# Decoder layer on one core: the last six attention pieces' places, the stores at the second set's end, and the time of the embedding's inputs

## The chip, the core and the metric

The kernel runs on one core of a Trainium2 chip. The core has five engines that each work through their own instructions in order: PE (TensorE, matrix products; PEld is its loading of weights), DVE (VectorE), ACT (ScalarE), POOL (GpSimd) and SP (SyncE, which here only issues DMAs; in the profile SPq). DMAs are issued by SP and by POOL. The metric is the device time of one execution in microseconds, lower is better.

## What is computed

One layer of a decoder on 1024 tokens of 2048 channels. Cut to what matters:

```python
h = x @ w_in + b_in                                # 2048 -> q, k, v, g_attn, u_pool, g_pool
q, k, v, g_attn, u_pool, g_pool = split(h)
a = banded_sink_attention(q, k, v, sinks, bias, valid) * silu(g_attn)
b = multiscale_pool(u_pool, w_pool, pool_scale) * silu(g_pool)
mix = concat([a, b]) @ w_out
ple = sigmoid(x @ w_gate_ple) * (p @ w_ple)        # p: 1024 x 256, the layer's embedding
out = layer_norm(ALPHA * x + mix + ple, ln_gain, ln_bias)
```

The attention looks back over 128 tokens, in blocks of 128 queries against 256 keys, with 16 heads of 64 channels; `ple` is the part for which the embedding's inputs `p` are needed. All inputs and outputs are float32.

## The kernel before

**Products.** All large matrix products are made by a scheme of seven products instead of eight for a 2 x 2 split of the blocks (`ALONE`, `BESIDE` give the order, p1 to p7). Each of the seven is one call of `product` (L464): four blocks of three matmuls (`mm3`, L180 to L186: high weights by high inputs, high by low, low by high), since float32 is split into a high and a low part. The product's weights are split by ACT (`wh`, the cast of L824) and by DVE (`wl`, the subtraction of L126), four products ahead (`take`, `units_to`), from a ring of five `raw` buffers that SP fills. For p5 and p6 DVE first makes sums and differences of the raw blocks (`three_sums`, `make_unit`). PE writes to the banks `qa` and `qb`, two of each; ACT copies a first result to a `part` tile (L424), DVE adds later ones to it (L126).

**The clock.** `run_group` counts a tick after each product. `after(n, fn)` puts `fn` into the program n products later, `later(n, fn)` does so behind the work that was marked last. So the order on each engine is fixed when the program is written, by these numbers; an engine that has to wait holds up all that stands behind it in its row.

**The sets.** The input projection is made in sets of groups for half of the input channels each: the first half's results go to DRAM as `h` (`keep`, store by SP through `load`, L139), and are added to the second half's by a DMA that POOL issues (`finished`, L432). Set 2 ends at about 675 us of the profiled execution; its last groups store `h_110` to `h_115`. Set 3 follows and takes the gate of the embedding in (`w_gate_ple`) too.

**Attention.** `heads` (L579) makes one of 16 pieces: two blocks (n = 0, 1) of two pairs of heads, spread over the products of set 2. Per block `score` (L620, eight matmuls `sc`), `softmax` (L639) and `share` (L649) on ACT, `trans` (L656, four transposes `tr`), a masked copy by POOL (L663), and `value` (L672, four matmuls `pv`, or two for a sequence's first block), whose two halves DVE adds. The pieces start nine products apart, the last six eight apart. With nine, one piece's `score` falls into the same place between two products as the `trans` and `value` of another; with eight they fall into four or five.

**Centred weights.** `centre_weights` (L947) reads the output weights as 32 cells of 256 KB (`cw`), subtracts a mean on DVE and stores them as `wc`, by SP; a later `cw` load waits for the store that frees its buffer.

**The embedding's inputs.** `embed_in` (L889) asks for four blocks of `p` at 1, 3, 5 and 7 products behind its start (DMA by SP, 256 KB, tile `s`, in_p), and nine behind it splits all four: a cast by ACT (L901) and a subtraction by DVE (L126, `self.lo`) each. The parts are used by `embed` (L913) about four products behind that. It is started in set 3 by

```python
            if self.groups[g + i + 1][0][0].b[0] == 4 and i < n3 - 2:
                self.after(5, self.embed_in)
```

Of the kernel before, what the change touches and what calls it, by code (L numbers as in the profile page):

```python
# [33 lines left out]
H = 4 * P  # L34
# [31 lines left out]
class Layer:  # L66
# [203 lines left out]
    def two(self):  # L270
        return self.tile(self.twos, [P, 2, self.F], "two")
# [304 lines left out]
        self.ident_act(c, c, self.b8[:, j : j + 1], 0.125)  # L576
        self.load(self.qd[j], c.rearrange("p h t -> p (h t)"))

    def heads(self, h, j, half):  # L579

        nc, g = self.nc, j // 4
        st = self.tile(self.sm, [P, 64], "st")
# [44 lines left out]
        def shift(n):  # L627
            f = slice(4 * n, 4 * n + 4)
            sink = self.c(C_SINK + 8 * j, 16).rearrange("p (i b e) -> p i b e", i=2, b=4)[:, :, block(n)]
            nc.vector.tensor_scalar(out=neg[:, f], in0=mx[:, f], scalar1=-1.0, scalar2=None, op0=ALU.mult)  # L630
            self.tt(sk[:, f].rearrange("p (i e) -> p i e", i=2), sink, neg[:, f].rearrange("p (i e) -> p i e", i=2), ALU.add)
            nc.scalar.activation(sk[:, f], sk[:, f], AF.Exp)
# [18 lines left out]
        def trans(n):  # L651
            ps = self.bank("tr", 1)
            for i in range(2):
                for e in range(2):
                    o = (2 * i + e) * P
                    nc.tensor.transpose(ps[:, o : o + P], sc[n, i][:, e, P:], self.ident)  # L656
            hi, lo = pt[n] = [self.slot(F32R)[:, :T] for _ in range(2)]
            nc.scalar.copy(out=hi, in_=ps)
            self.lo(lo, ps, hi)
            if not none(n):  # L660
                old[n] = [self.slot(F32R)[:, :T] for _ in range(2)]
                for a, t in zip(old[n], pt[n]):
                    nc.gpsimd.affine_select(out=a.rearrange("p (c q) -> p c q", c=4), in_=t.rearrange("p (c q) -> p c q", c=4).bitcast(F32), pattern=[[0, 4], [-1, P]],  # L663
                                            compare_op=ALU.is_ge, fill=0.0, base=-1, channel_multiplier=1)

        def value(n):
            ps = self.bank("pv", 1)
            ms = [(self.vv[h][:, block(n)], t) for t in pt[n]]
            if not none(n):
                ms += [(self.vd[h][:, block(n) - 1 + h], t) for t in old[n]]  # L670
            for i, (w, t) in enumerate(ms):
                nc.tensor.matmul(ps, w, t, start=i == 0, stop=i == len(ms) - 1)  # L672
            if not pre:
                pre.append(two(self.slot()[:, :T]))
            low = self.slot()[0:64, :T]
            nc.scalar.copy(out=low, in_=ps[64:128])
            hi, low = (t.rearrange("p (i e q) -> p i e q", i=2, e=2) for t in (ps[0:64], low))
            for e in range(2):
                self.tt(pre[0][64 * e : 64 * e + 64, :, n * P : n * P + P], hi[:, :, e], low[:, :, e], ALU.add)
            if n:  # L680
                f = slice(h * T + 256 * half, h * T + 256 * half + 256)
                for i in range(2):
                    (self.aside if last else self.load)(self.pre[j + i][:, f], pre[0][:, i])
# [4 lines left out]
        for n in range(2):  # L688
            for i in range(2):
                self.after(6 + 4 * n, lambda n=n, i=i: score(n, i))  # L690
            self.after(9 + 4 * n, lambda n=n: shift(n))
            self.after(15 + 4 * n, lambda n=n: trans(n))
            for i in range(2):
                self.after(10 + 4 * n, lambda n=n, i=i: softmax(n, i))
                self.later(12 + 4 * n, lambda n=n, i=i: share(n, i))
            self.after(19 + 5 * n, lambda n=n: value(n))


    def gate_ahead(self, j):
# [247 lines left out]
    def centre_weights(self, at, by):  # L947

        nc = self.nc
        cells = [(b, h) for b in range(NB) for h in range(2)]  # L950
        sums = self.fix.tile([P, 8, NB], F32, name="wsum")
        mean = self.fix.tile([P, 8], F32, name="wmean")
        now, cws = [], [self.cw, self.cw2]

        def fetch(b, h):
            cws.append(cws.pop(0))
            now.insert(0, self.load(self.tile(cws[0], [P, H], "cw"), self.wout[b, 0][:, h * H : h * H + H]))

        def add_up(b, h):
            k = now.pop().rearrange("p (k m) -> p k m", k=4)  # L960
            nc.vector.reduce_sum(sums[:, 4 * h : 4 * h + 4, b : b + 1], k, axis=mybir.AxisListType.X)

        def take_mean():
            nc.vector.reduce_sum(mean.rearrange("p (k b) -> p k b", b=1), sums, axis=mybir.AxisListType.X)
            nc.vector.tensor_scalar(out=mean, in0=mean, scalar1=1.0 / D, scalar2=None, op0=ALU.mult)

        def centre(b, h):
            w = now.pop()
            k = w.rearrange("p (k m) -> p k m", k=4)
            m = mean[:, 4 * h : 4 * h + 4].rearrange("p (k m) -> p k m", m=1).broadcast_to([P, 4, P])  # L970
            self.tt(k, k, m, ALU.subtract)
            self.load(self.wc[b, 0][:, h * H : h * H + H], w)

        for step in (add_up, centre):
            for c in cells:
                self.after(at, lambda c=c: fetch(*c))
                self.later(at + 3, lambda c=c, step=step: step(*c))
                at += by if step is centre and c[0] % 3 else 2
            if step is add_up:
                self.later(at + 2, take_mean)  # L980
                at += 2
# [114 lines left out]
    def run(self):  # L1096
# [29 lines left out]
        flat = lambda c: c.rearrange("p h t -> p (h t)")  # L1126
        halves = lambda t: t.rearrange("p (h t) -> p h t", h=2)
        store = lambda w: hid if w is win else gat
# [4 lines left out]
        def keep(where):  # L1133
            return lambda b, c: self.load(where[b], flat(c))

        def kept_part(where):
            return lambda b: halves(where[b])
# [19 lines left out]
        def jobs(todo, half, first, done, tokens=2 * T, ahead=None):  # L1157
            return [Job(w, b0, b1, half, first(w), done(w), tokens, ahead=ahead) for w, b0, b1 in todo]

        s1 = jobs(qkv, 0, lambda w: None, lambda w: keep(hid))  # L1160
        s2 = jobs(qkv, 1, lambda w: kept_part(hid), lambda w: finish)
        s2 += jobs(rest, 1, lambda w: None, lambda w: keep(store(w)))
        s3 = jobs(rest, 0, lambda w: kept_part(store(w)), consume)
        for j in s3:
            j.wait = 8 if j is s3[-1] else 7 if j is s3[-2] else 5 if j in s3[-4:] else 4
# [144 lines left out]
        t = 9  # L1310
        self.after(5, lambda: build_kv(KB, self.k_build, 0))
        self.after(6, lambda: build_kv(VB, self.v_build, 0))
        for i in range(16):
            self.after(t - 2 + 9 * i - max(0, i - 10), lambda i=i: self.heads(i // 2 % 2, i // 4 * 2, i % 2))
        for h, n in enumerate((65, 77)):
            self.after(t + n, lambda h=h: build_kv(KB, self.k_build, 1, (h,)))
        for h in range(2):
# [11 lines left out]
        for i in range(n3):  # L1329
            if i == 1:  # L1330
                over.close()
                work.close()
                work, over = ExitStack(), ExitStack()
                self.slot_n = T + 16
                self.slots = self.work_pool("slots", 16, work)
                self.extras = self.work_pool("e2", 6, over)
            if self.groups[g + i + 1][0][0].b[0] == 4 and i < n3 - 2:
                self.after(5, self.embed_in)
                self.after(7, lambda: self.embed_w(2))
            if i == n3 - 2:  # L1340

                over.close()
                work.close()
                work = ExitStack()
                self.slot_n = T
                six[:] = 5 * [pp] + 3 * [self.work_pool("p8", 3, work)]
                self.slots = self.work_pool("slots1", 8, work)
                self.twos = self.work_pool("twos1", 4, work)
                self.new_part = part_of_six
                for n, b in enumerate(s3[-4].b + s3[-3].b):  # L1350
                    self.after((1, 1, 5, 6)[n], lambda b=b: self.gate_ahead(b - GA0))
                pooled()
                for n, step in enumerate(make_pooled):
                    (self.later if n > 4 else self.after)((10, 13, 16, 19, 22, 27, 30)[n], step)
                for n, b in enumerate(b for j in s3[-2:] for b in j.b):
                    self.after(16 + 2 * n, lambda b=b: self.gate_ahead(b - GA0))
            first = self.groups[g + i][0][0]
            if first.w is wgate and first.b[0] in (4, 6, 8, 10):
                self.pool_sums(*divmod(first.b[0] // 2 - 2, 2), kept_pool)
            self.run_group(g + i, () if i else steps)  # L1360
# [3 lines left out]
        half = F1 // 2  # L1364
# [181 lines left out]
```

## Time and profile before

| | us |
|---|---|
| median of 3 runs | 1440.29 |
| lowest, highest | 1440.24, 1440.69 |
| profiled execution, its own time | 1439.74 |
| span of its profile | 1438.0 |
| PE busy | 1425.3 |
| DVE busy | 1114.3 |
| ACT busy | 791.4 |
| POOL busy | 234.5 |
| mean granted clock of PE | 0.996 |

The span goes from the first to the last instruction, all times below are counted from its start. A row of the timeline has start, duration, engine, line, operation, output<-input and count, and in brackets the idle time ahead of it with what ended it. The rows of issues have, per kind of DMA, the count, the size and the median time from issue to landing.

### The profile page before, as it was taken

Reading aid. Unit: us, or ns where it says so; the run is one execution under the profiler, and the core shown is the slowest. Engines: PE = TensorE matmul, PEld = TensorE weight load, DVE = VectorE, ACT = ScalarE, POOL = GpSimd, SP = SyncE. Lnnn points to the kernel's source line nnn. Section 1 sums busy time; section 2 is a strip of 40 time slices with the busy share of each in tenths; the row PEclk is TensorE's granted clock in tenths of the full one; section 3 lists DMA queues with packets and bytes.
Section 4 is the critical chain, followed back from the end, with each engine's and each line's share of the span. In section 5 each row is a group of like instructions: output and inputs, shape, how many; then the busy total and the mean of one; then the engine's idle time right before and its main releaser. Section 6 shows DMA issues by size and latency. Waiting matters only on the chain.

```text
span 1438.0 us, 20364 instructions
## 1 busy us (share of the span) xinstructions
PE 1425.3 (99%) x6824; PEld 1207.9 (84%) x6824; DVE 1114.3 (77%) x2044; ACT 791.4 (55%) x1564; POOL 234.5 (16%) x342
## 2 busy tenths in 40 slices
PE   9999999999999999999999999999999999999996
PEld 7888888888888888888888888888888888899996
DVE  7859578878888887887778876957677666987787
ACT  6546377565766666666565444443455533655476
POOL 0000202211221221221011211211000211111223
PEclk9999999999999999999999999999999999999998
DMA  9463886555556555548787869998799677494476
GB/s 360 186 239 117 235 227 212 168 182 170 173 187 205 192 182 190 193 149 282 207 248 216 222 205 292 341 279 255 201 300 314 193 204 230 134 280 117 117 238 232
DMA packets 119034, 311.86 MB, mean 217 GB/s; under 512 B 13585, under 2 KB 27025, under 8 KB 118929
## 3 DMA queue, kind: packets, MB, share of 16 engines
q1 hardware_dynamic: 94192, 229.82, 46.7%
q0 software_dynamic: 21408, 73.41, 21.6%
q10 hardware_dynamic: 3328, 7.34, 1.5%
q8 instruction: 53, 0.87, 0.3%
q14 instruction: 53, 0.43, 0.1%
HBM read 211.95 MB, written 98.57 MB: 216 GB/s over the span
## 4 chain that ended last, share of the span: by engine, by line
PE 98%; POOL 0%; ACT 0%; issue 0%; DMA 0%; DVE 0%; POOLq 0%; SPq 0%; DVEq 0%; ACTq 0%
PE qa L183 17%; PE qa L185 16%; PE qa L184 16%; PE qb L183 12%; PE qb L185 12%; PE qb L184 12%; PE sc L620 2%; PE pv L672 2%; PE sc L185 1%; PE sc L183 1%; PE sc L184 1%; PE tr L656 1%; PE tr L877 1%; PE pv L877 1%; DMA two<-in_p 0%
## 5 line engine op out<-in xcount | busy, mean ns | idle before, releaser
L824 ACT CAST wh<-raw 128x512 fp32r<-128x512 f32 x428 | 264.7, 620 | 412.3 <-PE qa L184 147.2
L126 DVE TENSOR_TENSOR wl<-raw,wh 128x512 fp32r<-128x512 f32 x428 | 295.9, 695 | 109.1 <-ACT wh L824 104.0
L424 ACT COPY part<-qa 128x512 f32<-128x512 f32 (+1 forms) x180 | 103.7, 576 | 82.4 <-PE qa L185 81.1
L126 DVE TENSOR_TENSOR part<-part,qb 128x512 f32<-128x512 f32 (+1 forms) x120 | 81.1, 676 | 48.6 <-PE qb L185 43.1
L183 PE MATMUL qa<-b11h,wh 128*128 128x512 f32 (+2 forms) x292 | 109.0, 373 | 0.0
L183 PE MATMUL qb<-b21h,wh 128*128 128x512 f32 (+2 forms) x292 | 108.9, 373 | 0.0
L185 PE MATMUL qa<-b11h,wl 128*128 128x512 f32 (+2 forms) x292 | 108.7, 372 | 0.0
L184 PE MATMUL qa<-b11l,wh 128*128 128x512 f32 (+2 forms) x292 | 108.5, 372 | 0.0
L185 PE MATMUL qb<-b21h,wl 128*128 128x512 f32 (+2 forms) x292 | 108.5, 372 | 0.0
L184 PE MATMUL qb<-b21l,wh 128*128 128x512 f32 (+2 forms) x292 | 108.4, 371 | 0.0
L183 PE MATMUL qb<-t1h,wh 128*128 128x512 f32 (+1 forms) x260 | 100.3, 386 | 0.0
L183 PE MATMUL qa<-t2h,wh 128*128 128x512 f32 (+1 forms) x260 | 100.0, 385 | 0.0
L183 PE MATMUL qa<-t3h,wh 128*128 128x512 f32 (+1 forms) x260 | 100.0, 385 | 0.0
L183 PE MATMUL qa<-t4h,wh 128*128 128x512 f32 (+1 forms) x260 | 99.8, 384 | 0.0
L185 PE MATMUL qb<-t1h,wl 128*128 128x512 f32 (+1 forms) x260 | 99.7, 384 | 0.0
L183 PE MATMUL qb<-b22h,wh 128*128 128x512 f32 (+1 forms) x260 | 99.7, 384 | 0.0
L185 PE MATMUL qa<-t2h,wl 128*128 128x512 f32 (+1 forms) x260 | 99.7, 383 | 0.0
L185 PE MATMUL qa<-t3h,wl 128*128 128x512 f32 (+1 forms) x260 | 99.7, 383 | 0.0
L185 PE MATMUL qb<-b22h,wl 128*128 128x512 f32 (+1 forms) x260 | 99.7, 383 | 0.0
L185 PE MATMUL qa<-t4h,wl 128*128 128x512 f32 (+1 forms) x260 | 99.6, 383 | 0.0
L184 PE MATMUL qb<-t1l,wh 128*128 128x512 f32 (+1 forms) x260 | 99.5, 383 | 0.0
L184 PE MATMUL qb<-b22l,wh 128*128 128x512 f32 (+1 forms) x260 | 99.5, 383 | 0.0
(336 smaller groups left out, 3488.8 us busy)
## 6 DMA issues: line engine op xcount, KB each, us to landing
raw<-in_win SPq DMA_DIRECT2D x65, 512.0 KB, 4.3
h<-part SPq DMA_DIRECT2D x34, 512.0 KB, 3.5
part<-h POOLq DMA_DIRECT2D x34, 512.0 KB, 7.0
cw<-in_wout SPq DMA_DIRECT2D x64, 256.0 KB, 3.3
raw<-in_wgate SPq DMA_DIRECT2D x32, 512.0 KB, 5.0
raw<-wc SPq DMA_DIRECT2D x32, 512.0 KB, 4.4
s<-in_x SPq DMA_DIRECT2D x44, 256.0 KB, 6.0
s<-in_rel SPq DMA_DIRECT2D x32, 256.0 KB, 3.8
```

Of the source, the lines that this page charges most:

```text
L126: return (eng or self.nc.vector).tensor_tensor(out=out, in0=a, in1=b, op=op)
L183: mm(ps, wh, xh, start=start, stop=False, skip_group_check=True)
L184: mm(ps, wh, xl, start=False, stop=False, skip_group_check=True)
L185: return mm(ps, wl, xh, start=False, stop=stop, skip_group_check=True)
L424: self.mark("ACT", self.nc.scalar.copy(out=dst, in_=ps))
L620: nc.tensor.matmul(ps[:, e, z:], q, kk[:, keys], start=k == 0, stop=k == 1)
L656: nc.tensor.transpose(ps[:, o : o + P], sc[n, i][:, e, P:], self.ident)
L672: nc.tensor.matmul(ps, w, t, start=i == 0, stop=i == len(ms) - 1)
L824: ins = self.nc.scalar.copy(out=out, in_=a)
L877: mm = self.nc.tensor.matmul(ps[b], w[u][:, b, k], self.ple_p[v][:, 2 * h + k], start=k + u + v == 0, stop=k + v == 2, skip_group_check=True)
```

## The change

Three edits. `heads` gets a fourth argument `by`, the distance to the next piece: nine for pieces 0 to 9, where nothing changes (15 and 19 products, 19 and 24 come out as before), eight for the last six: `trans` at 14 and 18 products instead of 15 and 19, `value` at 18 and 22 instead of 19 and 24. The stores of the last three groups of set 2 (`h_110` to `h_115`, 512 KB each) and of the last four cells of `wc` (256 KB each) are issued by POOL (`aside`) instead of SP (`load`). And `embed_in` starts three products ahead in place of five, so that its loads and its splits come two products sooner.

```diff
-    def heads(self, h, j, half):
+    def heads(self, h, j, half, by):
...
-            self.after(15 + 4 * n, lambda n=n: trans(n))
+            self.after(by + 6 + 4 * n, lambda n=n: trans(n))
...
-            self.after(19 + 5 * n, lambda n=n: value(n))
+            self.after(by + 10 + (by - 4) * n, lambda n=n: value(n))
...
-            self.load(self.wc[b, 0][:, h * H : h * H + H], w)
+            (self.aside if (b, h) in cells[28:] else self.load)(self.wc[b, 0][:, h * H : h * H + H], w)
...
         s2 += jobs(rest, 1, lambda w: None, lambda w: keep(store(w)))
+        for j in s2[-3:]:
+            j.done = lambda b, c, where=store(j.w): self.aside(where[b], flat(c))
...
-            self.after(t - 2 + 9 * i - max(0, i - 10), lambda i=i: self.heads(i // 2 % 2, i // 4 * 2, i % 2))
+            self.after(t - 2 + 9 * i - max(0, i - 10), lambda i=i: self.heads(i // 2 % 2, i // 4 * 2, i % 2, 9 - (i > 9)))
...
-                self.after(5, self.embed_in)
+                self.after(3, self.embed_in)
```

The changed file has two lines more behind L1162, so the lines that the rows name stay as they are.

On PE, at the first of the last six pieces, between two products of set 2 (`qa`, `qb`; the numbers are those of the tiles), in the program before:

```order
L185 MATMUL qa_5159<-t4h_1519,wl_5279 128x512
L672 MATMUL pv_5395<-s_5213,v_986_4708 128x512
L672 MATMUL pv_5395<-s_5214,v_986_4708 128x512
L672 MATMUL pv_5395<-s_5217,d_987_4709 128x512
L672 MATMUL pv_5395<-s_5218,d_987_4709 128x512
L656 MATMUL tr_5406<-ident,s_5088 128x128 x2
L656 MATMUL tr_5406<-ident,s_5096 128x128 x2
```

and in the changed one, one product sooner:

```order
L185 MATMUL qb_5282<-b22h_1475,wl_5252 128x512
L656 MATMUL tr_5345<-ident,s_5088 128x128 x2
L656 MATMUL tr_5345<-ident,s_5096 128x128 x2
L620 MATMUL sc_5369<-kh_1771,s_5272 128x256
L620 MATMUL sc_5369<-kl_1772,s_5272 128x256
```

The four transposes (two rows of two) of the shares `s_5088` and `s_5096` have moved from behind the value product to the place ahead of it, where another piece's scores stand.

On POOL, at the end of set 2, in the program before (the masked copies, the last attention results `pre`, and set 3's first instruction):

```order
L663 AFFINE_SELECT s_6836<-s_6832 128x512
L663 AFFINE_SELECT s_6958<-s_6954 128x512
L663 AFFINE_SELECT s_6959<-s_6955 128x512
L145 DMA pre_162<-s_6944 128x256
L145 DMA pre_163<-s_6944 128x256
L724 MEMSET s_7536 128x16
```

and in the changed one, from the second of the four `wc` stores on:

```order
L145 DMA wc_244<-cw_6796 128x512
L663 AFFINE_SELECT s_6939<-s_6935 128x512
L663 AFFINE_SELECT s_6940<-s_6936 128x512
L145 DMA wc_245<-cw_6899 128x512
L145 DMA h_112<-part_6697 128x1024
L145 DMA h_114<-part_6699 128x1024
L145 DMA wc_245<-cw_6960 128x512
L145 DMA pre_162<-s_6925 128x256
L145 DMA pre_163<-s_6925 128x256
L145 DMA h_113<-part_6698 128x1024
L145 DMA h_115<-part_6700 128x1024
L724 MEMSET s_7536 128x16
```

The stores of `wc` and `h` have come into POOL's row between its last masked copies and the results `pre`; on SP they are gone.

On ACT, in set 3, where the embedding's inputs are split (e and s from L901 are their high parts, the tiles right of the arrow the inputs; `wh` are weights, `part` copies of PE's results), in the program before:

```order
L154 CAST s_9137<-s_9041 128x512
L824 CAST wh_9165<-raw_8741 128x512
L424 COPY part_9047<-qa_9052 128x512
L901 CAST e_9216<-s_8999 128x512
L824 CAST wh_9189<-raw_8741 128x512
L824 CAST wh_9241<-s_1880_9184 128x512
L901 CAST e_9220<-s_9066 128x512
L424 COPY part_9239<-qa_9245 128x512
L901 CAST s_9228<-s_9160 128x512
L901 CAST e_9224<-s_9113 128x512
```

and in the changed one:

```order
L154 CAST s_9139<-s_9043 128x512
L901 CAST e_9162<-s_8960 128x512
L824 CAST wh_9181<-raw_8741 128x512
L901 CAST e_9166<-s_9001 128x512
L901 CAST s_9174<-s_9115 128x512
L901 CAST e_9170<-s_9068 128x512
L424 COPY part_9049<-qa_9054 128x512
L424 COPY part_9239<-qa_9245 128x512
L824 CAST wh_9205<-raw_8741 128x512
L824 CAST wh_9241<-s_1888_9200 128x512
```

The four casts of L901 (fourth input: `s_9160` before, `s_9115` now) have moved from behind the copy of `part_9047` to ahead of the corresponding copy, of `part_9049`, the fourth right behind the second.

On DVE at the same place, in the changed program, the subtractions of the inputs and what follows:

```order
L126 TENSOR_TENSOR e_9167<-s_9001,e_9166 128x512
L126 TENSOR_TENSOR s_9175<-s_9115,s_9174 128x512
L126 TENSOR_TENSOR e_9171<-s_9068,e_9170 128x512
L927 SCALAR_TENSOR_TENSOR part_8839<-s_9028,part_8839 128x512
L126 TENSOR_TENSOR wl_9182<-raw_8741,wh_9181 128x512
L126 TENSOR_TENSOR part_9048<-part_9048,qb_9123 128x512
```

Then an addition to `part`, a sum of `raw` and a multiplication (L927) follow, and on to the `wl` of a p6 product (`wl_9206`, used by PE with `t2h`):

```order
L126 TENSOR_TENSOR raw_8898<-raw_8741,raw_8898 128x512
L126 TENSOR_TENSOR s_9088<-s_9090,s_9088 128x512
L126 TENSOR_TENSOR raw_8741<-s_1888_9200,raw_8741 128x512
L126 TENSOR_TENSOR s_9090<-s_9094,s_9090 128x512
L126 TENSOR_TENSOR raw_8741<-raw_8741 128x512
L126 TENSOR_TENSOR wl_9206<-raw_8741,wh_9205 128x512
```

Thirteen rows go from the subtraction of the fourth input (`s_9175`) to `wl_9206`; before, the subtractions of the inputs stood behind the corresponding `wl_9190`. On SP the fourth input's load stands behind the same two weight loads as before, and waits for the addition of `s_9032` to `part_8839` on DVE.

## Prediction

> **What bounds the kernel now.** I read the page's busy times first, then the chain of work that ended last, then the timeline of the matrix engine at the places that the change touches.
>
> ```profile
> PE 1425.3 (99%) x6824; PEld 1207.9 (84%) x6824; DVE 1114.3 (77%) x2044; ACT 791.4 (55%) x1564; POOL 234.5 (16%) x342
> PE 98%; POOL 0%; ACT 0%; issue 0%; DMA 0%; DVE 0%; POOLq 0%; SPq 0%; DVEq 0%; ACTq 0%
> ```
>
> PE is busy for 1425.3 us, 99% of the span, and carries 98% of the chain. So time is won only where PE's work gets shorter or one of its few gaps closes, and it is lost only where something makes PE wait: any such wait goes into the end one for one. A product is 12 matmuls; how far apart these stand is seen from the first and the third of one.
>
> ```profile
> 913.47 0.39 PE L183 MATMUL qa<-t2h,wh 128*128 128x512 f32 x1
> ...
> 913.92 0.39 PE L185 MATMUL qa<-t2h,wl 128*128 128x512 f32 x1
> ```
>
> (913.92 − 913.47) / 2 = 0.225 us, so 2.7 us a product. The third matmul is the first that reads `wl`, DVE's half of the weights.
>
> **Part 1, the joined places.** The first ten attention pieces already have their scores, transposes and value products at two places of PE's stream, the last six at four or five. The trace has both kinds with the same work between their ends: 96 matmuls of products, 16 of scores, 8 transposes, 8 value matmuls.
>
> ```profile
> 485.08 0.63 PE L672 MATMUL pv<-s,v 128*128 128x512 f32 x2
> 511.60 0.28 PE L620 MATMUL sc<-kh,s 128*128 128x256 f32 x1
> 604.25 0.28 PE L620 MATMUL sc<-kh,s 128*128 128x256 f32 x1
> 630.89 0.28 PE L620 MATMUL sc<-kh,s 128*128 128x256 f32 x1
> ```
>
> Joined: 511.60 − 485.08 = 26.52 us. Apart: 630.89 − 604.25 = 26.64 us. Joining saves 0.12 us per eight products. Places apart stand from 511.60 to 630.89, 119.29 / 26.64 = 4.5 such stretches: 0.54 us, and with the shorter pieces at the end about **0.6 us gained**. At worst it is nothing, if a joined place has to wait for its inputs, so I looked whether they are there.
>
> ```profile
> 614.55 1.28 ACT L649 ACTIVATE s<-s,st 128x128 f32<-128x128 f32 x4
> 621.28 0.60 PE L656 MATMUL tr<-ident,s 128*128 128x128 f32 x4
> ```
>
> The shares that the transposes read end at 615.83 and the transposes start at 621.28. One product earlier they still have 5.45 − 2.7 = 2.7 us. The second value product comes two products earlier, but four products behind its transposes, as the first one always did.
>
> **Part 2, two gaps that DVE makes.**
>
> ```profile
> 643.93 0.39 PE L185 MATMUL qb<-b21h,wl 128*128 128x512 f32 x1
> 644.26 0.47 PE L183 MATMUL qb<-t1h,wh 128*128 128x512 f32 x1
> 644.57 0.39 PE L184 MATMUL qb<-t1l,wh 128*128 128x512 f32 x1
> ...
> 686.03 0.39 PE L185 MATMUL qb<-b21h,wl 128*128 128x512 f32 x1
> 686.34 0.47 PE L183 MATMUL qb<-t1h,wh 128*128 128x512 f32 x1
> 686.65 0.39 PE L184 MATMUL qb<-t1l,wh 128*128 128x512 f32 x1
> ```
>
> The two steps take 0.64 and 0.62 us instead of 2 x 0.225: 0.19 + 0.17 = 0.36 us lost. PE waits there for a bank that DVE empties late.
>
> ```profile
> 643.43 0.68 DVE L126 TENSOR_TENSOR part<-part,qb 128x512 f32<-128x512 f32 x1
> 685.52 0.68 DVE L126 TENSOR_TENSOR part<-part,qb 128x512 f32<-128x512 f32 x1
> ```
>
> They end at 644.11 and 686.20, behind PE's wish of 644.16 and 686.26 only by the hand-over. In the new order one value's additions leave DVE's queue two products earlier, and one operation ahead of each of the two is enough to close a gap of 0.2 us. I count 0.36 us gained; the bounds are 0 (they stay) and twice as much lost (two new ones like them). **Sum of parts 1 and 2: −0.96 us.**
>
> **Part 3, POOL's stores at the end of the second set.** SP gives up the last stores of `h` and four of `wc`.
>
> ```profile
> 671.19 5.67 SPq L140 DMA_DIRECT2D h<-part  x4
> 678.72 1.11 POOL L145 DMA_DIRECT2D pre<-s  x2 [15.21 <-DVE s L126]
> 680.00:700.00 20.00, 20.00 (x89) 16.34 (x88) 18.77 (x31) 14.89 (x28) 0.00 (x0) 1.00 0.64 226
> ```
>
> SP is held there 5.67 us, but PE is busy for 20.00 of the 20 us behind it: freeing SP wins nothing. What could be lost is time until the buffers come free. No row has these stores on POOL; the nearest are POOL's stores of 512 KB at the kernel's end and SP's of `wc`; then the places that depend on them:
>
> ```profile
> wc<-cw SPq DMA_DIRECT2D x32, 256.0 KB, 2.7
> co<-part POOLq DMA_DIRECT2D x16, 512.0 KB, 6.4
> 682.38 0.57 ACT L424 COPY part<-qa 128x512 f32<-128x512 f32 x1
> 655.33 5.96 SPq L140 DMA_DIRECT2D raw<-in_win  x3
> 675.36 0.40 PE L183 MATMUL qa<-b11h,wh 128*128 128x512 f32 x1
> ```
>
> Asked for at about 671, a store is down at 671 + 6.4 = 677.4; the copy at 682.38 is the first to write into its buffer, 5 us later. The weights issued from 655.33 now stand behind two loads that wait for `wc` stores on POOL; 6.4 − 2.7 (SP's median for `wc`) = 4 us later at most, and they are used at 675.36. Cost taken: 0; if a store took over 11.4 us, each further one goes into the end.
>
> [...]
>
> **Part 4, the embedding's inputs, decides.** The four loads, casts and subtractions come two products sooner. The loads have these neighbours, each row of issues with its time to landing under it:
>
> ```profile
> 899.94 0.86 SPq L140 DMA_DIRECT2D raw<-in_wgate  x2
> DMA to landing us min/median/max: 6.3/6.8/7.2
> 903.17 0.33 SPq L140 DMA_DIRECT2D s<-in_p  x1
> DMA to landing us min/median/max: 5.0/5.0/5.0
> s<-in_p SPq DMA_DIRECT2D x4, 256.0 KB, 6.8
> DMA  9999999999997499999999999999999999999998
> ```
>
> The fourth input is asked for at 903.17 behind two weights (900.47 + 7.2 = 907.7) and lands at 903.17 + 5.0 = 908.2 (the median of the four is 6.8); the last row, the DMA engines' busy tenths from 870 to 910, is nearly all nines. In the program of the change this input stands on SP **behind the same two weights**, and its buffer is now freed by the addition of `part` and `s` that DVE has here:
>
> ```profile
> 903.66 0.68 DVE L126 TENSOR_TENSOR part<-part,s 128x512 f32<-128x512 f32 x1
> ...
> 918.10 1.28 DVE L126 TENSOR_TENSOR wl<-raw,wh 128x512 fp32r<-128x512 f32 x2
> ```
>
> So the request does not come two products sooner: it goes out at 903.66 + 0.68, about 904.4. Only its use comes sooner. The landing is 904.4 + 5.0 = 909.4 if it takes as long as before, 904.4 + 2.7 = 907.1 by the shortest row quoted for 256 KB (SP's `wc` stores), and 908.2 if it comes right behind the weights, as it does now. I take **908.2**, the middle.
>
> Before, the casts stood behind a copy at 908.23, so nothing waited for the landing:
>
> ```profile
> 908.23 0.59 ACT L424 COPY part<-qa 128x512 f32<-128x512 f32 x1 [4.99 <-PE qa L185]
> 908.71 0.63 ACT L901 CAST e<-s 128x512 fp32r<-128x512 f32 x1
> ```
>
> Now the casts stand in what was ACT's idle time of 4.99 us, from 903.2 on, and at the fourth it stands until 908.2. That alone costs little. But DVE comes to the fourth subtraction at 903.66 + 3 x 0.602 = 905.5 and stands too, with 13 steps from there to the `wl` of the product at 913.47. DVE's step in this stretch is (918.10 − 903.66) / 24 = 0.602 us without a pause, so nothing is made up. The subtraction starts at 908.2 + 0.63 for the cast + about 0.1 = 908.95; 13 x 0.602 = 7.83 later, at 916.8, `wl` starts and is done after 0.68 at 917.5. PE wants it at 913.92: **PE waits 3.6 us**, of which the bank and weight waits of the products between are part. A landing at 907.1 gives 2.5, one at 909.4 gives 4.8. Without any wait for the input the same count from 905.5 ends at 914.0, a wait of 0.1.
>
> [...]
>
> **Sum** against the profiled execution: 1439.74 − 0.96 + 3.6 = 1442.4. The median of the runs is 1440.29, 0.55 above that execution: **1442.9 us**. A measurement of this kernel can tell some 0.2% from no change, 2.9 us: slower starts at 1443.2, faster at 1437.4.
>
> **Rivals.**
> *The input is in time* (the first three loads, earlier now, empty the queue; or DVE reaches the releasing addition sooner): the wait is 0.1 to 2 us. For it: the 2.7 us of the stores. Against it: DMA engines that are full. Without the wait 1440.29 − 0.96 + 0.1 = 1439.4, with 2 us 1441.3. Chance 0.2. It turns the sign where the wait falls below 0.96 us, a landing before 905.6.
> *The input comes late*: as late as the median of all four, 6.8 us, it lands at 911.2 and PE waits 6.6: 1445.9. From 909.4 on every us counts whole. Against it: it was the fastest of the four in its old place. Chance 0.12.
> *The stores hold up the third set*: POOL's stores take 14 us instead of 6.4 and the copy at 682.38 waits 14 − 11.4 = 2.6 us, beside the stall of part 4: 1445.5. Chance 0.08.
> *Nothing of the joins comes true* (DVE's gaps stay, new ones come): 0.96 more, inside the range.
>
> **How the numbers follow.** Forecast, a wait of 2.5 to 4.8: 0.60, 1441.8 to 1444.1 us. Something under half of it lies beyond 1443.2, with the two late cases: slower 0.25 + 0.19 = 0.44. Faster needs 3 us that no part offers: 0.02. Same: 0.54. The range goes from the case in time, 1439.4, to 1445.0, between the forecast's upper end and the two late cases, which it leaves out in the main: some 0.15.
>
> **What would show it.** PE: one gap of 2.5 to 4.8 us at or just ahead of the product at 913, with `wl` or `wh` named as releaser; ACT idle for some 4 us ahead of a cast of L901, released by a DMA; the fourth input's landing behind the weights. Two places with transposes per eight products from 511 to 675, and a stretch of 26.5 us. No gap at 644 and 686. No wait of the copy near 682. Wrong would be: no gap near 913 (the landing), or a second gap elsewhere in the third set (the stores).

## The result, and the profile after

The changed kernel takes 1451.16 us (median of 6 runs, 1448.89 to 1452.36), the kernel before 1440.26 on the same chip: a ratio of 1.0075, interval 1.0062 to 1.0088. It is 10.9 us slower; the forecast was 1442.9 and its range ended at 1445.0. The profiled execution took 1452.36 us, the slowest of the six, with a span of 1450.6.

First the page of the changed kernel: busy times, and the chain of work that ended last.

```profile
PE 1429.4 (99%) x6824; PEld 1210.3 (83%) x6824; DVE 1112.6 (77%) x2044; ACT 791.1 (55%) x1564; POOL 238.7 (16%) x352
PE 94%; DMA 3%; issue 2%; DVE 1%; POOL 0%; ACT 0%; SPq 0%; POOLq 0%; DVEq 0%; ACTq 0%
```

PE's work is the same, but it is busy for 4.1 us more, and 6% of the chain is not PE, where it was 2%. Then the view of waits, for PE: who waited for whom, us in total, times, longest.

```profile
PE qb L183 <- ACT b22h L824: 3.9, 1, 3.9
PE qa L183 <- ACT wh L824: 2.4, 1, 2.4
...
PE sc L185 <- DVE s L126: 0.8, 1, 0.8
PE qa L183 <- ACT part L424: 0.7, 1, 0.7
```

These four are the largest that the kernel before does not have: 7.8 us. Where they are, and what comes behind them, is in PE's timeline and in the view of windows (from:to, length, then busy time of PE, PEld, DVE, ACT, POOL with instructions, PE's granted clock, DMA share, GB/s).

```profile
679.04 0.50 PE L183 MATMUL qa<-b11h,wh 128*128 128x512 f32 x1 [0.73 <-ACT part L424]
691.42 0.76 PE L183 MATMUL qb<-t1h,wh 128*128 128x512 f32 x1 [3.93 <-ACT b22h L824]
...
924.13 0.50 PE L183 MATMUL qa<-t2h,wh 128*128 128x512 f32 x1 [2.36 <-ACT wh L824]
```

```profile
684.00:691.40 7.40, 3.49 (x16) 2.57 (x15) 5.12 (x9) 7.09 (x15) 0.00 (x0) 0.90 1.05 397
691.40:696.80 5.40, 5.38 (x13) 4.24 (x14) 4.69 (x8) 3.40 (x8) 0.00 (x0) 0.51 0.11 39
...
924.10:928.70 4.60, 4.57 (x13) 3.32 (x13) 4.60 (x9) 1.54 (x3) 1.11 (x2) 0.64 1.03 219
```

Two things were not in the forecast. At the end of set 2, where the stores moved and the cost was put at nothing, PE waits at 679 and at 691. And behind each long wait PE runs one product at a granted clock of 0.51 or 0.64: twelve steps from one matmul to the next take 5.26 us (691.42 to 696.68) and 4.57 us (924.13 to 928.70) instead of 2.72. The wait at 924 is the one that was forecast, at the place and with the releaser that were named.

What holds PE at 679 and 691 is read in ACT's timeline:

```profile
677.88 0.62 ACT L824 CAST t1h<-s 128x512 fp32r<-128x512 f32 x1 [0.62 <-DMA s<-t]
678.40 0.58 ACT L424 COPY part<-qa 128x512 f32<-128x512 f32 x1
...
679.75 0.62 ACT L824 CAST t2h<-s 128x512 fp32r<-128x512 f32 x1 [0.24 <-DMA s<-t]
681.51 0.62 ACT L824 CAST t2h<-s 128x512 fp32r<-128x512 f32 x1 [1.14 <-DMA s<-t]
683.51 0.62 ACT L824 CAST t2h<-s 128x512 fp32r<-128x512 f32 x1 [1.38 <-DMA s<-t]
684.04 0.58 ACT L424 COPY part<-qa 128x512 f32<-128x512 f32 x1
684.51 0.62 ACT L824 CAST wh<-s 128x512 fp32r<-128x512 f32 x1
...
685.84 1.99 ACT L824 CAST t3h<-s 128x512 fp32r<-128x512 f32 x3 [0.19 <-DMA s<-t]
...
688.21 0.62 ACT L824 CAST t3h<-s 128x512 fp32r<-128x512 f32 x1
...
690.29 0.62 ACT L824 CAST wh<-raw 128x512 fp32r<-128x512 f32 x1
```

The casts that split set 3's inputs (t1, t2, t3) stand for their loads, and behind them stand the copy that frees PE's bank and the casts of PE's next weights. The copy at 678.40 ends PE's wait at 679. For the product at 691 the last weight cast is the one at 690.29, behind those of t3; PE's loading of weights waits 4.3 us for a weight cast there, and the cast of b22 that the row of PE names stands right behind it and is no input of this product. The profile before has the copy at 682.38 with the first t2 cast behind it. The rows of the two programs show that the order itself was changed. Before:

```
L424 COPY part_6677<-qa_6732 128x512
L676 COPY s_7082<-pv_7077 64x512
L824 CAST wh_7151<-s_1470_7146 128x512
L424 COPY part_7088<-qa_7120 128x512
L824 CAST wh_7180<-s_1476_7175 128x512
L424 COPY part_7090<-qa_7155 128x512
L824 CAST t2h_7228<-s_7102 128x512
L824 CAST t2h_7228<-s_7104 128x512
```

and in the changed kernel:

```
L424 COPY part_6700<-qa_6732 128x512
L824 CAST wh_7116<-raw_6987 128x512
L824 CAST t2h_7228<-s_7102 128x512
L824 CAST t2h_7228<-s_7104 128x512
L824 CAST t2h_7228<-s_7106 128x512
L424 COPY part_7088<-qa_7120 128x512
L824 CAST wh_7151<-s_1470_7146 128x512
L824 CAST t2h_7228<-s_7108 128x512
```

No line of the diff touches these casts. In SP's row, without its stores, the last eight of twelve loads of t now follow the first four at once, and in the program that is built the casts stand earlier in ACT's row; how the build comes to that order is not shown here. But most of the loads land no sooner. From the rows of SP's queue, and of the issues from 640 to 700 us with their time to landing, in the changed kernel:

```profile
667.80 10.44 SPq L140 DMA_DIRECT2D s<-t  x12
s<-t SPq DMA_DIRECT2D x16, 256.0 KB, 9.0
h<-part POOLq DMA_DIRECT2D x4, 512.0 KB, 7.6
```

and the same kind in the kernel before, where four stores of `h` and one of `wc` stood on SP between the first four and the next eight:

```profile
s<-t SPq DMA_DIRECT2D x16, 256.0 KB, 5.8
```

Load by load, from the issue and its own time to landing: the first four are asked for 1.6 to 1.9 us later than before and land 1.6 to 3.7 us later. The next eight are asked for 3.5 to 7.2 us sooner; two of them land 2.4 and 1.4 us sooner, the others between 0.2 us sooner and 0.4 later. The stores are on their way beside them, and the DMA engines are full (1.05 in the window from 684.00). That the stores are what slows the loads fits this, but no run separates it.

At the embedding the place and the last links of the forecast hold. The issue of the fourth input with its time to landing, the fourth cast on ACT, the subtraction and the late `wl` on DVE:

```profile
L140 SPq DMA_DIRECT2D s<-in_p x1: 328/328/328, 908.7 to 908.7; - x1
DMA to landing us min/median/max: 7.2/7.2/7.2
```

```profile
916.01 0.62 ACT L901 CAST s<-s 128x512 fp32r<-128x512 f32 x1 [4.05 <-issue]
```

```profile
916.66 0.69 DVE L126 TENSOR_TENSOR s<-s,s 128x512 fp32r<-128x512 f32 x1 [2.73 <-ACT s L901]
...
924.48 0.70 DVE L126 TENSOR_TENSOR wl<-raw,wh 128x512 fp32r<-128x512 f32 x1
```

The input lands at 908.7 + 7.2 = 915.9, ACT stands 4.05 us for it and DVE 2.73, and from the subtraction to the start of `wl` it is 924.48 − 916.66 = 7.82 us, thirteen steps, as worked out (7.83).

### The profile page after: what moved, and what is told of

Same layout as the page of the kernel before. It is cut to its first block, busy times and chain, and to the rows that moved or that the text cites. A ratio compares the mean times of both kernels' runs of the same rounds, so it can differ in the third digit from the quotient of the medians.

```text
span 1450.6 us, 20393 instructions
## 1 busy us (share of the span) xinstructions
PE 1429.4 (99%) x6824; PEld 1210.3 (83%) x6824; DVE 1112.6 (77%) x2044; ACT 791.1 (55%) x1564; POOL 238.7 (16%) x352
## 4 chain that ended last, share of the span: by engine, by line
PE 94%; DMA 3%; issue 2%; DVE 1%; POOL 0%; ACT 0%; SPq 0%; POOLq 0%; DVEq 0%; ACTq 0%
PE qa L183 16%; PE qa L185 16%; PE qa L184 16%; PE qb L183 12%; PE qb L185 12%; PE qb L184 12%; PE sc L620 2%; PE pv L672 2%; PE sc L185 1%; PE sc L183 1%; PE sc L184 1%; DMA s<-t 1%; PE tr L656 1%; DMA s<-in_p 1%; PE tr L877 1%
## 5 line engine op out<-in xcount | busy, mean ns | idle before, releaser
L184 PE MATMUL qa<-t2l,wh 128*128 128x512 f32 (+1 forms) x260 | 100.0, 385 | 0.0
```

The lines of the kernel that those rows point to most:

```text
L184: mm(ps, wh, xl, start=False, stop=False, skip_group_check=True)
```

## The experiments

All were timed against the kernel before on the same chip; times are medians. The first four take the change apart. The theory by then: three separate losses, the order of ACT's row at the end of set 2, the embedding's input, and the slow product behind each long wait.

### Joined places alone

```diff
-            self.after(15 + 4 * n, lambda n=n: trans(n))
+            self.after(by + 6 + 4 * n, lambda n=n: trans(n))
...
-            self.after(19 + 5 * n, lambda n=n: value(n))
+            self.after(by + 10 + (by - 4) * n, lambda n=n: value(n))
```

> The kernel before with the first edit only (the last six pieces' places). In the trace of the changed kernel the product at 675 stands 0.75 us earlier against before than the product at 510 did, so theory and rivals agree here: 0.75 us faster than before (1439.5), no gap at 644 and 686 over 0.1 us, no wait of PE between 670 and 700. If the stall of the changed kernel at 679 to 697 came from the joined places and not from the stores, this run would show it: 7 us slower, about 1447.

Measured: 1441.81 us (1439.86 to 1443.47) against 1440.89, ratio 1.0005 (0.9996 to 1.0014). Half of the expectation fell: there is a wait at the end of set 2 with the joins alone too. The profile caught one of the slowest runs; PE and ACT, and SP's queue, there:

```profile
680.77 0.50 PE L183 MATMUL qa<-b11h,wh 128*128 128x512 f32 x1 [2.23 <-ACT part L424]
```

```profile
679.10 0.62 ACT L824 CAST t1h<-s 128x512 fp32r<-128x512 f32 x1 [4.95 <-DMA s<-t]
679.62 0.61 ACT L824 CAST wh<-raw 128x512 fp32r<-128x512 f32 x1
680.14 0.58 ACT L424 COPY part<-qa 128x512 f32<-128x512 f32 x1
```

```profile
670.64 2.13 SPq L140 DMA_DIRECT2D h<-part  x2
673.04 0.32 SPq L140 DMA_DIRECT2D wc<-cw  x1
673.46 2.62 SPq L140 DMA_DIRECT2D s<-t  x4
```

With the joins the first four loads of t stand behind two stores on SP (673.46; before, 666.23, ahead of them), and one t1 cast ahead of a copy on ACT. So the joins have a loss of their own, by the same kind of mechanism; it seems to come and go between runs, since the fastest, 1439.86, has no room for it, but only one run has a profile.

### Without the embedding's edit, and without the stores

```diff
-                self.after(3, self.embed_in)
+                self.after(5, self.embed_in)
```

> The changed kernel with the embedding's inputs asked for at the old time. Theory: the stores cost 0.9 us of waiting at 679, 4.0 at 691 and 2.4 us in which the product behind it runs at a granted clock of about 0.5, so 7.3 - 0.75 = 6.6 us above before, 1446.8, the wait at 691 stays at 3.9, the gap at 924 (now near 921) is gone. Rival: the two stalls hang together, the second is only the first one's echo; then both are as before and the time stays near 1451.

Measured: 1445.60 (1444.41 to 1446.50), ratio 1.0028 (1.0017 to 1.0038). The wait near 921 is gone; the one at 691 stays with 3.3 us, and one of 1.2 us is at the copy near 680. So the two stalls do not hang together. In sum it is 4.7 us above before instead of 6.6.

```diff
-            (self.aside if (b, h) in cells[28:] else self.load)(self.wc[b, 0][:, h * H : h * H + H], w)
+            self.load(self.wc[b, 0][:, h * H : h * H + H], w)
...
-        for j in s2[-3:]:
-            j.done = lambda b, c, where=store(j.w): self.aside(where[b], flat(c))
```

> The changed kernel with all ten stores by SP again (joined places and embedding edit stay). Theory: no wait at 679 and 691, one wait near 914 of 2.5 to 3 us and 1.85 us more in the slow product behind it, 0.8 us at 885 if that belongs to the embedding: 4.5 to 5.3 - 0.75 above before, 1444.0 to 1444.8. Rival, the embedding's stall is an echo of the first: 1439.5.

Measured: 1445.93 (1445.24 to 1446.78), ratio 1.0034 (1.0022 to 1.0047). That is 5.0 above before, where 3.8 to 4.6 were expected. The wait at 691 is gone with the stores; one of 1.0 us at a copy stays, as with the joins alone, which fits the excess. The embedding's stall is there in full.

### The casts held in ACT's row

This is the test of the mechanism. The loads and stores are asked for as the change has them; the order on ACT is set back, by letting the casts of t1, t2 and t3 issue, in the whole program, behind what ACT had been given three or four products before (`marks` keeps the last instruction of each engine after every product).

```diff
+    def behind(self, lag):
+        ctx = ExitStack()
+        for e, ins in self.marks[-lag].items() if lag else ():
+            if e in ('ACT',):
+                ctx.enter_context(self.tc.issue_after(ins))
+        return ctx
...
-            for n in range(2):
-                self.split_part(u, n, pieces[n])
+            with self.behind({'t1': 3, 't2': 3, 't3': 4}.get(u)):
+                for n in range(2):
+                    self.split_part(u, n, pieces[n])
```

> The changed kernel, stores by POOL, but the casts of t1, t2 and t3 are held in ACT's row behind the copies and weight casts of three to four products before them, where they stood before; the loads and stores stay as they are. Theory (the stall comes from ACT's row: casts moved ahead of copies and weights stand there for loads that land no sooner than before): waits at 679 and 691 under 0.5 us in sum, no slow product there, the embedding's stall stays: 1444 to 1445. Rival, the stores by POOL hold the part buffers or the loads land too late beside them: the wait at 691 stays at 3 us or more, 1449 or above.

Measured: 1444.09 (1442.75 to 1445.82), ratio 1.0023 (1.0014 to 1.0032). PE's waits that are new against before, and the loads from 640 to 700 us, in this kernel (its lines are ten further on):

```profile
PE qa L191 <- ACT wh L834: 2.4, 1, 2.4
...
PE qb L193 <- DVE wl L126: 0.7, 1, 0.7
```

```profile
s<-t SPq DMA_DIRECT2D x16, 256.0 KB, 9.2
```

Both waits are at the embedding; none is left at the end of set 2. The loads are as late as in the changed kernel, 9.2 us, and the stores still go by POOL. So the late loads and the stores by POOL do not make the stall by themselves; it needs the place of the casts in ACT's row.

### What is left without the embedding's loss, or with its loads sooner

Both keep the stores by POOL, the joins and the held casts. The first takes the embedding back to its old time. The second keeps the early splits and asks for the inputs one product apart:

```diff
-                self.after(1 + 2 * i, lambda i=i: r.append(self.fetch(self.p[i // 2][:, i % 2])))
+                self.after(1 + i, lambda i=i: r.append(self.fetch(self.p[i // 2][:, i % 2])))
```

> Joined places and stores by POOL, the casts of t1 to t3 held in ACT's row, the embedding's inputs at the old time. In the run with the casts held the PE stream gained 0.9 us by the product at 834 and lost all the rest at the embedding (3.6 us of waiting, 1.9 in the slow product behind it). Theory: without the embedding's edit 0.6 to 1.2 us faster than before, no wait of PE between 600 and 1000 us over 0.5. Rival: some of the loss has a third source in set 3: then not faster than before.

> All edits, casts held, and the four loads of the embedding's inputs issued 1, 2, 3 and 4 products behind the start instead of 1, 3, 5 and 7; the splits stay at nine, where the change has them. The fourth load now stands ahead of the two weight loads and its buffer is freed by an addition about three products earlier. Theory (DVE and ACT stood for a landing): the input is down by 905, PE waits 0 to 0.3 us near 914, time as with the old embedding, 0.6 to 1.2 us faster than before. Rival (DVE has too many rows ahead of the weights there, whatever the landing): the wait near 914 stays at 2 us or more and the time at 1443 to 1444.

Measured: 1439.19 with the old embedding (ratio 0.9992, 0.9983 to 1.0001), 1439.23 with the loads sooner (0.9990, 0.9981 to 0.9999), against 1440.53: 1.3 us faster each, at the edge of what can be told. In the second PE's whole list of waits is

```profile
PE sc L1075 <- POOL st L126: 1.1, 1, 1.1
PE tr L1112 <- PEq L1550: 0.8, 1, 0.8
PE pv L1047 <- ACT t2l L1038: 0.2, 1, 0.2
```

and none of it lies in set 2 or 3: with the input there in time, the early splits cost nothing. DVE's load was not the cause; the landing was. No run holds the casts alone, so how much of the 1.3 us comes from the joins and how much from the hold is not shown.

### Stores alone, and joins held without the stores

> The kernel before with the ten stores by POOL only. In ACT's row the four t2 casts then stand ahead of one copy and one weight cast behind which they stood before, the t1 casts hardly move. Theory: PE waits 1 to 4 us at one place between 680 and 692 and the product behind it is slow if the wait is over 2 us: 1441.5 to 1446. Rival (the stall needs both edits): like before within 0.5 us.

Measured: 1442.00 (1440.63 to 1443.81), ratio 1.0010 (1.0001 to 1.0019), against 1440.53. In the profiled execution, one of the fastest (1440.81), PE waits 0.3 us twice:

```profile
PE qb L183 <- DVE part L126: 0.3, 1, 0.3
PE qa L183 <- ACT part L424: 0.3, 1, 0.3
```

The median is 1.5 us above before, inside what was expected, but these waits are shorter than expected, and the slower runs have no profile. A wait of more than 3 us at this place was seen only with both edits.

The next is the joins alone with the casts held as above, stores by SP.

> Joined places alone, stores by SP as before, and the casts of t1 to t3 held. With the joins alone, the copy at 680 stood behind a t1 cast that waited for a load which SP issued behind two stores. Theory (ACT's row makes the wait): no wait of PE from 670 to 700 over 0.5 us, 0.6 to 1.2 us faster than before, so the stores by POOL are not needed. Rival (the loads behind SP's stores are too late for the products themselves): a wait of 1 us or more between 680 and 692 stays, time at 1441 to 1443.

Measured: 1439.39 (1438.55 to 1440.68), ratio 0.9992 (0.9983 to 1.0001): as expected, 1.1 us faster, and without any wait of PE between 600 and 1000 us in its list. The stores by POOL are not needed.

### What a wait costs behind its own end

```diff
+        for _ in range(14 if i == 90 else 0):
+            self.nc.scalar.copy(out=hi, in_=src)
         cast = self.copy(hi, src)
```

> The kernel before with one weight cast done 14 times more (0.52 us each) ahead of one product of set 2, so that PE stands for that one weight and for nothing else. It measures what a wait costs behind its own end. Theory (granted clock): a wait up to about 1.2 us costs itself and 0.2 us more at most, one over 2 us costs about 2 us more, in the one product behind it, at a granted clock of 0.5 to 0.65, whatever its length. This one should be 0 to 2 us long. Rival (the products behind the two stalls were slow because their own weights or banks were late): here the product behind the wait takes its usual 2.72 us after a wait of any length.

> The same with 18 casts more: a wait some 2 us longer than with 14. Theory: if it is over 2 us, the product behind it takes 1.7 to 2.4 us more than 2.72. Rival: 2.72.

> The same with 26 casts more: a wait some 6 us long. Theory: the product behind it takes 1.7 to 2.5 us more than 2.72, not more than with 18, and later ones 2.72 again. Rival: 2.72; second rival, the loss grows with the wait: 4 us or more.

These lines make one weight cast of the kernel before late. One run each: 1441.59, 1444.30 and 1454.42 us against 1440.96. The window of the 12 matmuls behind the wait, with 14, 18 and 26 casts:

```profile
288.90:291.70 2.80, 2.80 (x12) 2.22 (x13) 2.80 (x5) 1.53 (x3) 0.00 (x0) 1.00 0.78 241
```

```profile
292.60:297.00 4.40, 4.40 (x12) 3.47 (x13) 4.40 (x12) 1.98 (x6) 1.37 (x2) 0.61 0.52 148
```

```profile
300.60:305.20 4.60, 4.59 (x12) 3.62 (x13) 4.50 (x7) 1.62 (x3) 0.00 (x0) 0.59 0.38 114
305.20:308.00 2.80, 2.80 (x14) 2.29 (x13) 1.40 (x3) 1.13 (x3) 0.00 (x0) 1.00 0.30 118
```

Behind a wait of 0.5 us the product takes 2.8 us at full clock. Behind 8.2 us it takes 4.6 at 0.59, 1.9 more, and the next is normal: no more than behind the waits of 2.2 to 3.9 us, so the price does not grow with the wait. The middle run answered otherwise than set out:

```profile
289.96 0.50 PE L674 MATMUL pv<-s,v 128*128 128x512 f32 x1 [1.57 <-ACT s L660]
...
292.59 0.50 PE L183 MATMUL qa<-t4h,wh 128*128 128x512 f32 x1 [0.70 <-ACT wh L826]
```

No wait in it is over 1.6 us, but three (1.6, 0.2, 0.7) lie within 4.2 us with 1.7 us of work between, and the product behind them is slow all the same. So, by this one run, short waits in a row seem to count together.

## Why the prediction failed, step by step

**Part 1, the joins: right, but not alone.** From the product that starts at 506.15 to the one at 675.36 the kernel before takes 169.21 us; the changed one 168.47, between the last two of these rows (the first is of before):

```profile
506.15 0.39 PE L183 MATMUL qa<-t3h,wh 128*128 128x512 f32 x1
...
506.95 0.39 PE L183 MATMUL qa<-t3h,wh 128*128 128x512 f32 x1
...
675.42 0.39 PE L183 MATMUL qa<-b11h,wh 128*128 128x512 f32 x1
```

That is 0.74 us less, where 0.6 for the joins and 0.19 for the gap at 644 were counted. What was not counted is that with the joins alone SP's first loads of t come to stand behind two of its stores, most likely since the value product, two products earlier, frees its tiles in another order; in the profiled execution that is a stall of 2.23 us.

**Part 2, the two gaps: right, where ACT's row is kept.** At 644 a joined place now stands, and the gap at 686 is gone with the joins and the casts held:

```profile
685.58 0.39 PE L193 MATMUL qb<-b21h,wl 128*128 128x512 f32 x1
685.81 0.39 PE L191 MATMUL qb<-t1h,wh 128*128 128x512 f32 x1
```

All in all the kernels with the joins, the casts held and no loss at the embedding gained 1.1 to 1.3 us where 0.96 was forecast.

**Part 3, the stores: this is the step that failed.** It said "Cost taken: 0", with the reason that freeing SP wins nothing and that buffers would come free in time. They did, and the rival of late stores was wrong as well (no run shows its 14 us, an assumption of the author): POOL's stores of `h` took 7.6 us, far from the 11.4 that would have cost something, and no engine waited for one between 660 and 700 us. What was left out is what comes of the other rows when SP's stores go: the loads of t follow each other sooner on SP, and in the program that is built the casts stand earlier on ACT. SP was read for what it delays, not for what it starts sooner. The order of ACT's rows around 680 shows it without a run; the prediction compared ACT's rows at the embedding only. Of the 12.6 us between the two profiled executions the end of set 2 has 7.45 (the product at 675.42 starts 0.06 us later than before, the one at 696.68 7.51 later than its like at 689.17): 0.73 + 3.93 in waits, the rest mainly the slow product behind the second. By the medians the stores cost 1.5 us alone (1442.00 − 1440.53), 3.8 beside the joins (1445.60 − 1441.81) and 5.9 beside both other edits (10.9 − 5.0). So the edits make each other worse; why the third adds to the cost of the stores was not followed up.

**Part 4, the embedding: right in place and in its last links, its landing right by luck, short in price.** The landing behind the weights, ACT and DVE standing, thirteen steps to `wl`: all there. But the request was not late because of its buffer. The addition that was taken to free it (903.66 before) stands here at

```profile
912.04 0.68 DVE L126 TENSOR_TENSOR part<-part,s 128x512 f32<-128x512 f32 x1
```

and the load of the fourth input had gone out at 908.7. The addition of its kind ahead of it, at 899.22 before and 907.21 here, gives the shift between the two executions, 8.0 us. By it the request came at 900.7 where 904.4 was forecast, 2.5 us sooner than before and not 1.2 later, and took 7.2 us to land where 3.8 was assumed. The two errors cancel: the landing, 907.9, is the 908.2 of the forecast by luck. The wait was forecast at 3.6 us; with the casts held it is 0.7 + 2.4 = 3.1 in the rows, and PE's stream falls back by 3.6 (from the product at 836.40 to the one at 916.54 it takes 80.14 us, before, from 836.88 to 913.47, 76.59). In the changed kernel, where PE was 0.8 us later already by another small wait, it is 2.4 to 2.7. But in the profiles the stall costs about 5.5 us in all, since the product behind it runs at a reduced clock (0.64 in the changed kernel). By the medians the embedding's edit costs 4.1 us beside the joins (1445.93 − 1441.81), 4.5 with the casts held (3.2 + 1.3) and 6.2 beside both other edits (10.9 − 4.7). Each wait was priced at its own length; 2.5 us of clock had to be added behind the wait at 691 and 1.9 behind the one at 924.

So the forecast of 1442.9 lacked two terms, both at work in the profile of the changed kernel: the reordered casts, and the clock. Without the first, the kernel with the casts held (1444.09) lies inside the range.

On the clock, the runs show a granted clock of 0.51 in the window from 691.40, behind a wait of 3.93 us, and a loss that does not grow with the wait (2.5 us behind 3.93, 1.9 behind 8.2); single waits of 2.2 and 2.4 us were enough for it. It bears on every forecast of a wait, and was not counted in this one.

## What to carry to other kernels

When an instruction leaves a queue, ask what that queue does next, and whether the rows of other engines have changed with it: work that has moved forward in the row of an engine that executes in order waits there for data that comes no sooner, as ACT's cast of t1 did for 4.95 us with the joins alone. Compare the rows of every engine at every place that the change touches, for casts or copies that now stand ahead of what the busiest engine waits for. And price a wait of PE that is over some 2 us (2.23 is the shortest single one with a slow product behind it here, 1.24 the longest without) at its length plus 1.5 to 2.5 us: that is what the product behind it lost in the seven stretches seen here (1.5 behind 3.3 us, 1.9 behind 8.2, 2.5 behind 3.93; the three short waits of the middle run count as one).

## What was not expected of the hardware

The granted clock falls behind a single wait of 2.23 us: in the kernel with the joins alone the twelve matmuls after it take 4.40 us.

```profile
680.80:685.20 4.40, 4.40 (x12) 3.51 (x13) 4.40 (x9) 2.53 (x5) 0.00 (x0) 0.61 0.93 342
```

Behind waits of 0.5 to 1.2 us it does not show: the twelve matmuls behind the 1.24 us of the kernel without the embedding's edit take 2.90 us (679.48 to 682.38). And loads issued 3.5 to 7.2 us sooner beside other transfers came, but for two of eight, no more than 0.2 us sooner: 9.0 us to landing instead of 5.8 in the median of all sixteen, with the DMA engines full (1.05 in the share of the window from 684.00 to 691.40).
